# Weight tiles that start at a moving 8-byte offset, in a two-layer diffusion block

## The chip, the cores and the metric

One core of a Trainium2 chip runs the whole program. The time is the device time of one execution in microseconds; of three runs the median is taken. TensorE (PE) does the matmuls, and its weight loads (PEld) are shown as a row of their own; VectorE (DVE), ScalarE (ACT), GpSimd (POOL) and SyncE (SP, which here issues the transfers) work beside it.

## The reference

Two layers over 512 latent tokens and 256 context tokens of width 1024, in float32. Each layer is a mixer between two half-step SwiGLU FFNs, each with RMSNorms and a shift, scale and gate from a modulation vector.

```python
x = sublayer_out(x, swiglu(sublayer_in(x, g[0], mx[0], mx[1]), ffn_w_in[i, 0], ffn_w_out[i, 0]), g[1], mx[2], 0.5)
...
def swiglu(h, w_in, w_out):
    gate, up = jnp.split(h @ w_in, 2, axis=-1)     # 1024 -> 2 x 2816
    return (jax.nn.silu(gate) * up) @ w_out        # 2816 -> 1024
```

The mixer of layer 0 is a bidirectional state-space scan (SSD) in 8 groups, that of layer 1 a gated MLP (gMLP) whose gate mixes the tokens of a chunk. The first FFN and the SSD run on the context too. All of it is dominated by products of activations and weights.

## The kernel before

Every product is made of three matmuls of type fp32r: an operand is split into a high part (a rounded copy, `S.copy` in line 111) and a low part (the rest, a subtraction in line 112), and high x high, high x low and low x high are added up in PSUM. `load_w` does this for weights: it fetches 512 KB into a `raw` tile, takes two weight tiles of 128 x 1024 from `w_tile`, one for each part, and calls `split`. `mm` (line 122) issues every matmul; its second argument is the stationary operand (loaded into the array by a weight load of its own before each matmul), its third the moving one.

There are two kinds of products. In the first halves of the FFNs (`ffn_in`, by `fm_mm`), the weights are stationary and the activations move: `uh` and `ul` hold high and low part of the 512 latent tokens (8 blocks of 512 columns, 2048 bytes each), `uch` and `ucl` those of the 256 context tokens. For each of 8 blocks `fm_mm` issues high weights x `uh`, high weights x `ul`, low weights x `uh`, so that 24 matmuls use one pair of weight tiles. In the second halves (`out_gen`) the weights move in halves of 512 columns, and the stationary operand is a slice of the split hidden activations, which lie in weight tiles too (`prep_h`).

```python
for k in range(KC):
    mm(ps, wh3[:, k], uhh[:, k, lo:hi], k == 0, False)
    mm(ps, wh3[:, k], ull[:, k, lo:hi], False, False)
    mm(ps, wl3[:, k], uhh[:, k, lo:hi], False, k == KC - 1)
```

`w_tile` takes the next entry of a ring. The ring (`extra_w`) runs through the 8 buffers of tag `w` in the pool `wp` and then through n buffers of tag `w2` in a pool of the stage, 8 in the later FFNs: four weight pairs from the one and four from the other, in turn. At the end of a stage, slots of the FFN pool's `hT` tiles are used as well.

SBUF is laid out by pools, one behind another from the left (`const`, `up` with `uh` and `ul`, `rawp`, `wp`, `smp` with small tiles, `chp`, then the pools of a stage) and some from the right (`ucp` with `uch` and `ucl`, the residual stream `x`). In front of all lie 16 KiB of scratch. The order of the work is that of the code, and is not touched. Worked out from the sizes in the code, the start of a tile in its partition, modulo 512 bytes, is:

| tiles | residue before | residue after |
|---|---|---|
| `uh`, `ul` | 384 | 0 |
| weight tiles in `wp` | 384 | 8 x (5n mod 64) |
| weight tiles in the FFN pools and the pools of the last projections | 192 | 8 x (5n mod 64) |
| the one extra weight buffer in the pool of gMLP | 288 | 96 more than the others |
| `uch`, `ucl` | 480 | 0 |

n counts the weight tiles in the order in which they are taken. A weight block of 128 columns is 512 bytes, so all blocks of a tile have its residue, and so have all slices of `uh` and `ul` that a matmul reads.

Of the kernel before, what the change touches and what calls it, by code (L numbers as in the profile page):

```python
# [8 lines left out]
F32 = mybir.dt.float32  # L9
F32R = mybir.dt.float32r  # L10
# [15 lines left out]
LAG = 4  # L26
BG = 4

# order of the work on one group of SSD heads: F a piece of the next group's projections, ct/cs the
# context's chunks and states, lt/ls a latent chunk's transposes and states, d/e its decays (next  # L30
# group), a1/a2/a3 its scores, output and transposed output, p2/p3/fin what the group before left
ORDER_FIRST = """
F lt0 lt1 F ct lt2 F d0 e0 lt3 cs a10 a11 F ls0 ls3 F ls1 ls2 a20 a12 d1 e1 d2 e2 a21 F F
F F a22 d3 e3 a3 a13
# [15 lines left out]
def build(tc, I, out, upto=99):  # L50
    nc = tc.nc
# [3 lines left out]
    def pool(name, bufs=1, space=None, stack=None, side="left"):  # L55
        kw = {"side": side} if space is None else {"space": space}
        if space is not DRAM:
            kw["reuse_waits"] = "tile"
        return (stack or es).enter_context(tc.tile_pool(name=name, bufs=bufs, **kw))

    const = pool("const")
    up = pool("up")
    rawp = pool("rawp")
    wp = pool("wp")
    smp = pool("smp")
# [5 lines left out]
    def nm(s):  # L71
        cnt[0] += 1
        return f"{s}_{cnt[0]}"

    def ps_tile(tag="ps", bufs=4):
        return psp.tile([128, 512], F32, tag=tag, name=nm("ps"), bufs=bufs)

    chp = pool("chp")

    def ja(shape=(128, 1024)):  # L80
# [6 lines left out]
        return smp.tile([128, n], F32, tag=f"sm{n}", name=nm("sm"), bufs=12)  # L87

    NW = 8
    ring = [None]  # L90

    def extra_w(p, n, first=()):
        ring[0] = chain(first, cycle([(wp, "w", NW)] * NW + [(p, "w2", n)] * n))

    def w_tile(shape=(128, 1024)):
        p, tag, n = next(ring[0])
        return p.tile(list(shape), F32R, tag=tag, name=nm("w"), bufs=n)

    raws = [None]

# [13 lines left out]
    def load_w(dram, shape=(128, 1024), eng=None):  # L114
        r = raw_tile(shape)
        Q.dma_start(out=r, in_=dram)
        h, l = w_tile(shape), w_tile(shape)
        split(r, h, l, eng)
        return h, l
# [4 lines left out]
    ones = const.tile([1, 128], F32, name="ones")  # L124
# [177 lines left out]
    def out_gen(src, nch, wdram, toks, post, tail=4, bgn=0, spilled=False, banks=None, inter=None, now=99, slots=None):  # L302
# [4 lines left out]
        def prep_h(cp):  # L307
            hh, hl = w_tile((128, 2, ntok)), w_tile((128, 2, ntok))
            if spilled and cp not in spilled:
                hs = raw_tile((128, 2, ntok))  # L310
                Q.dma_start(out=hs, in_=src[cp][:, :, t0:t0 + ntok])
            else:
                hs = src[cp][:, :, t0:t0 + ntok]
            split(hs, hh, hl)
            return hh, hl
# [43 lines left out]
    def ffn_in(wdram, uhh, ull, ntok, fpool, bgn, nhalf_pairs=2, inter=None, start=None, engs=(V, V)):  # L359
# [44 lines left out]
                inter.pop(0)()  # L404
        return hts

    ucstk = ExitStack()
    ucp = pool("ucp", stack=ucstk, side="right")
    uch = ucp.tile([128, KC, CTX], F32R, name="uch")
# [12 lines left out]
    def ssd(ph, posts):  # L422
        main = ExitStack()
        sp = pool("ssd", stack=main)
# [15 lines left out]
        arow = sp.tile([128, 64], F32, name="arow")  # L440
        Q.dma_start(out=arow, in_=I["alog"].to_broadcast([128, 64]))
        S.activation(arow, arow, AF.Exp)

        def tl(shape, tag, bufs, dt=F32):
            return sp.tile(list(shape), dt, tag=tag, name=nm(tag), bufs=bufs)

        # step sizes and decays; the running sums of the latent tokens, from the middle of each
        # chunk, are kept with the tokens on the partitions (colt) and along the rows (rowd)
        colt = tl((128, NT, 2, 32), "col", 1)
        rowd = drp.tile([1, 64 * SEQ], F32, name="rowd")  # L450

        def steps_mm(hh, ll, n):
            wdh, wdl = load_w(I["ssd_wdt"].rearrange("p (k m) -> p k m", k=KC), (128, KC, 64))
            ps = ps_tile()
            for k in range(KC):
                mm(ps[:64, :n], wdh[:, k], hh[:, k, :], k == 0, False)
                mm(ps[:64, :n], wdh[:, k], ll[:, k, :], False, False)
                mm(ps[:64, :n], wdl[:, k], hh[:, k, :], False, k == KC - 1)
            return ps
# [296 lines left out]
        o = next(gen)  # L756
        next(gen)
        s = steps(px, SEQ, True)
# [10 lines left out]
        s = steps(steps_mm(uch, ucl, CTX), CTX, False)  # L769
# [17 lines left out]
        def post1(t, ps2):  # L787
            return pre_norm(xt[t], pre[:, 0, 2], uh, ul, t, post_norm(ps2, xt[t], row))

        # output projection: the first channels for the first half of the tokens while the last  # L790
        # group is under way, the others for all tokens, then the first ones for the second half
        def out_proj(o):
            n1 = 12
            ps = [[ps_tile("ps") for h in range(2)] for t in range(2)]
# [1 line left out]
            def prep_h(cp, lo, hi):  # L796
                shape = (128, 2, hi - lo)
                hh, hl = w_tile(shape), w_tile(shape)
                if cp == o.g:
                    hs = o.yt  # L800
                else:
                    hs = raw_tile(shape)
                    Q.dma_start(out=hs, in_=yts[cp][:, :, lo:hi])
                split(hs, hh, hl)
                return hh, hl
# [46 lines left out]
        for g in range(NG):  # L852
            if g + 1 < NG:
# [5 lines left out]
                prev, o = o, nxt  # L859
# [24 lines left out]
        if upto == 2:  # L884
            dump()

    # first feature tiles of the first FFN, contraction outermost so that each slice of the
    # modulation vector is used as soon as it is known
    def first_pairs(fpool, scc):
        prev = [None]  # L890
        slots = cycle([(fpool, "hT", 11)] * 11 + [(cp_, "w2", 3)] * 3)
        ring[0] = repeat((wp, "w", NW))

# [80 lines left out]
        late.extend(lambda f=f, r=r: rest(f, r) for f, r in pending)  # L974
        return [(acc[2 * f], acc[2 * f + 1]) for f in range(3)]

# [1 line left out]
    with ExitStack() as ph:  # L978
        cp_ = pool("ctxp", stack=ph)
        extra_w(cp_, 3)  # L980
# [3 lines left out]
        first = first_pairs(fpool, scc)  # L984
# [25 lines left out]
        out_phase(hts, NFP, I["ffn_out"][0], range(NTC), postc, tail=4, now=0,  # L1010
                  slots=[(fpool, "hT", 11)] * 9 + [(cp_, "w2", 3)] * 3)

# [1 line left out]
    with ExitStack() as ph:  # L1014
        ssd(ph, posts)

# [126 lines left out]
def consts():  # L1143
    import numpy as np
    i = np.arange(128)
    t, j = i[:, None], i[None, :]
    # the last two sum from the middle of a chunk, so that differences of sums lose less
    m = [t == j, t <= j, t >= j, t > j, t < j, t >= 0 * j,
         1 * ((t >= 64) & (t <= j)) - 1 * ((t > j) & (t < 64)), 1 * ((t >= j) & (t < 64)) - 1 * ((t >= 64) & (t < j))]
    return np.concatenate([np.broadcast_to(z, (128, 128)) for z in m], 1).astype(np.float32)  # L1150


def layout(inputs):
# [6 lines left out]
    R["ctx"] = A["ctx"].reshape(CTX, D)  # L1160
    R["c_ctx"] = A["c_ctx"].reshape(1, D)
    R["consts"] = consts()
    R["ada"] = A["ada_w"].transpose(0, 2, 1).reshape(2, 72, 128, D)
    R["cols"] = np.concatenate([
# [36 lines left out]

def program(arrays, upto=99):
    import concourse.bacc as _bacc
    nc = _bacc.Bacc("TRN2", target_bir_lowering=False, num_devices=1)
    I = {k: nc.dram_tensor(f"in_{k}", v.shape, mybir.dt.from_np(v.dtype), kind="ExternalInput").ap()
         for k, v in arrays.items()}
    out = nc.dram_tensor("out_0", (SEQ, D), F32, kind="ExternalOutput").ap()
    with tile.TileContext(nc) as tc:
        build(tc, I, out, upto)
    return nc  # L1210
# [8 lines left out]
```

## Time and profile before

| what | value |
|---|---|
| runs | 2600.75, 2601.16, 2601.23 us (median 2601.16) |
| span of the profiled execution | 2597.1 us |
| that execution's time | around its span, some 4 us; the page gives the span |
| TensorE, matmuls | 2537.9 us busy (98%), 12729 instructions |
| TensorE, weight loads | 2118.4 us (82%) |
| VectorE, ScalarE, GpSimd | 1535.7 us (59%), 986.4 us (38%), 339.9 us (13%) |
| mean of the granted TensorE clock | 0.995 |
| data moved | 359.09 MB, mean 138 GB/s |

The stages follow one another: the first FFN on latent tokens and then on the context to about 610 us, the SSD to 1210 us, FFN to 1560, FFN to 1940, gMLP to 2230 and the last FFN to the end. Matmuls are pipelined: one is drawn from its start until its last result, so durations overlap, and the pace is read from starts.

### The profile page before, as it was taken

The numbers are of one execution on the slowest core, as the hardware profiler recorded it, in microseconds if no ns is written. First come the engines' busy times: TensorE is split into PE (matmuls) and PEld (weight loads), VectorE is DVE, ScalarE is ACT, GpSimd is POOL, SyncE is SP. The second block draws the span as 40 slices with busy tenths as digits, with TensorE's granted clock in tenths as the row PEclk, the third lists the DMA queues.
The fourth block names the chain that finished last, engine by engine and source line by source line (L and its number), as shares of the span: only waits on it lengthen the run. The fifth ranks groups of instructions, "written<-read, shape, count | busy, mean of one in ns | idle before, by whom it ended". The sixth has DMA issues, their size and how long they took to land.

```text
span 2597.1 us, 32686 instructions
## 1 busy us (share of the span) xinstructions
PE 2537.9 (98%) x12729; PEld 2118.4 (82%) x12729; DVE 1535.7 (59%) x2224; ACT 986.4 (38%) x1464; POOL 339.9 (13%) x442
## 2 busy tenths in 40 slices
PE   5999999999899999999999999999999999999999
PEld 3888889988788888778888888888888788888887
DVE  8875547557989989977654346542342744522333
ACT  3422326446545455546222234222243323422222
POOL 5000001001545554420000000000010100000000
PEclk9999999999999999999999999999999999999999
DMA  5566545654432332345765344752333224222231
GB/s 199 191 202 206 170 146 181 201 174 138 123 91 101 97 102 90 118 162 198 238 202 168 130 130 140 234 170 73 109 111 106 81 92 136 90 98 90 81 99 63
DMA packets 131806, 359.09 MB, mean 138 GB/s; under 512 B 12234, under 2 KB 48514, under 8 KB 131652
## 3 DMA queue, kind: packets, MB, share of 16 engines
q1 hardware_dynamic: 131364, 356.82, 42.0%
q8 instruction: 100, 1.64, 0.3%
q14 instruction: 54, 0.44, 0.1%
q10 hardware_dynamic: 288, 0.19, 0.0%
HBM read 348.41 MB, written 8.55 MB: 137 GB/s over the span
## 4 chain that ended last, share of the span: by engine, by line
PE 82%; DVE 8%; DMA 3%; POOL 3%; ACT 2%; issue 1%; SPq 0%; POOLq 0%; DVEq 0%; ACTq 0%
PE ps L122 80%; DMA R<-rowd 2%; DVE acc L536 2%; DVE w L112 1%; DVE wm L671 1%; POOL R L619 1%; PE ps L269 1%; DVE ub L932 1%; POOL xs L559 0%; DVE ex L624 0%; DMA raw<-in_ssd_out 0%; POOL y L689 0%; DVE ub L570 0%; ACT w L111 0%; DVE ub L569 0%
## 5 line engine op out<-in xcount | busy, mean ns | idle before, releaser
L122 PE MATMUL ps<-uh,w 128*128 128x512 f32 (+1 forms) x3792 | 1155.1, 385 | 10.2 <-ACT uh L953 7.6
L112 DVE TENSOR_TENSOR w<-raw,w 128x1024 fp32r<-128x1024 f32 (+2 forms) x463 | 560.2, 1217 | 519.9 <-ACT w L111 342.6
L122 PEld LDWEIGHTS ps<-uh,w 128*128 128x128 f32 x3792 | 704.4, 189 | 155.3 <-ACT uh L953 8.8
L111 ACT CAST w<-raw 128x1024 fp32r<-128x1024 f32 (+2 forms) x471 | 482.1, 1032 | 905.1 <-PE ps L122 620.8
L122 PE MATMUL ps<-w,w 128*128 128x512 f32 x3144 | 729.5, 392 | 1.7 <-DVE w L112 1.5
L122 PE MATMUL ps<-ul,w 128*128 128x512 f32 (+1 forms) x1896 | 727.2, 384 | 2.6 <-DVE ul L954 2.6
L122 PEld LDWEIGHTS ps<-w,w 128*128 128x128 f32 x3144 | 587.7, 188 | 132.7 <-DVE w L112 2.8
L122 PEld LDWEIGHTS ps<-ul,w 128*128 128x128 f32 x1896 | 359.1, 189 | 78.0 <-DVE ul L954 4.8
L182 DVE CUSTOM_DVE_ANT_0 raw<-raw,sc 128x1024 f32<-128x1024 f32 x128 | 156.7, 1224 | 151.4 <-DMA raw<-in_ada 150.8
L239 POOL TENSOR_TENSOR sm<-sm,neghalf 128x1 f32<-128x1 f32 x26 | 7.2, 276 | 1601.3 <-ACT ja L237 1601.3
L122 PE MATMUL ps<-uch,w 128*128 128x256 f32 x1104 | 208.9, 286 | 0.0
L122 PEld LDWEIGHTS ps<-uch,w 128*128 128x128 f32 x1104 | 172.2, 188 | 2.6 <-issue 1.9
L122 PE MATMUL ps<-w,uh 128*128 128x256 f32 (+1 forms) x768 | 173.2, 320 | 0.0
L122 PE MATMUL ps<-ucl,w 128*128 128x256 f32 x552 | 155.6, 282 | 0.0
L536 DVE SCALAR_TENSOR_TENSOR acc<-ps,cw,acc 128x511 f32<-128x511 f32 (+2 forms) x224 | 138.5, 626 | 21.9 <-ACT acc L532 21.8
L372 DVE TENSOR_TENSOR hT<-ps,sil 128x512 f32<-128x512 f32 (+1 forms) x110 | 69.8, 634 | 112.4 <-PE ps L122 102.6
L122 PEld LDWEIGHTS ps<-w,uh 128*128 128x128 f32 x768 | 127.6, 190 | 10.4
L112 DVE TENSOR_TENSOR w<-hT,w 128x1024 fp32r<-128x1024 f32 (+1 forms) x63 | 71.2, 1130 | 96.2 <-ACT w L111 75.5
L122 PE MATMUL ps<-w,ul 128*128 128x256 f32 (+1 forms) x384 | 122.4, 319 | 0.0
L111 ACT CAST w<-hT 128x1024 fp32r<-128x1024 f32 (+1 forms) x63 | 61.1, 973 | 151.2 <-PE ps L122 151.2
L122 PEld LDWEIGHTS ps<-ucl,w 128*128 128x128 f32 x552 | 103.2, 187 | 2.0 <-issue 1.4
L371 ACT ACTIVATE sil<-ps 128x512 f32<-128x512 f32 (+1 forms) x110 | 60.8, 552 | 94.4 <-PE ps L122 94.4
(196 smaller groups left out, 1862.5 us busy)
## 6 DMA issues: line engine op xcount, KB each, us to landing
raw<-in_ffn_in SPq DMA_DIRECT2D x214, 512.0 KB, 3.8
raw<-in_ada SPq DMA_DIRECT2D x128, 512.0 KB, 4.3
raw<-in_ffn_out SPq DMA_DIRECT2D x110, 512.0 KB, 3.3
raw<-in_ssd_w SPq DMA_DIRECT2D x32, 512.0 KB, 4.5
R<-rowd SPq DMA_DIRECT2D x64, 256.0 KB, 5.0
raw<-in_ssd_out SPq DMA_DIRECT2D x28, 512.0 KB, 3.4
st<-in_ada SPq DMA_DIRECT2D x16, 512.0 KB, 7.3
raw<-in_ssd_z SPq DMA_DIRECT2D x16, 512.0 KB, 3.3
```

The source lines that it names most:

```text
L111: S.copy(out=h, in_=src)
L112: (eng or V).tensor_tensor(out=l, in0=src, in1=f32(h), op=ALU.subtract)
L122: T.matmul(o, a, b, start=start, stop=stop)
L182: V.tensor_tensor_reduce(out=r, in0=r, in1=sc, op0=ALU.mult, op1=ALU.add, scale=1.0, scalar=0.0, accum_out=mods[:, l, f:f + 1])
L239: G.tensor_tensor(out=v[:, 0:1], in0=ss[:, 0:1], in1=epsd, op=ALU.add)
L269: T.transpose(out=pt[:, k * 128:(k + 1) * 128], in_=xr[:, kk * 128:(kk + 1) * 128], identity=ident)
L371: S.activation(sil, pg[:, :ntok], AF.Silu)
L372: a = V.tensor_tensor(out=hts[-1][:, f % 2, :], in0=pu[:, :ntok], in1=sil, op=ALU.mult)
L536: V.scalar_tensor_tensor(out=acc[:, lo:hi], in0=ps[:, lo + sh:hi + sh], scalar=cw[:, j, k:k + 1], in1=acc[:, lo:hi], op0=ALU.mult, op1=ALU ...
L619: G.tensor_tensor(out=R[d], in0=R[d], in1=colt[:, c, d, gs][:, :, None].to_broadcast([128, 4, 128]), op=ALU.subtract)
L671: V.scalar_tensor_tensor(out=w1[:, h], in0=ge, scalar=sx["dt"][:, 1, c, 4 * g + h:4 * g + h + 1], in1=w1[:, h], op0=ALU.mult, op1=ALU.add)
L932: V.tensor_tensor_reduce(out=ub(), in0=r, in1=sc, op0=ALU.mult, op1=ALU.add, scale=1.0, scalar=0.0, accum_out=m0[:, f:f + 1])
```

## The change

`w_tile` allocates 128 elements (512 bytes) more than a tile needs and hands out a slice that begins o elements into the buffer, with o = 2 x (5n mod 64), that is at a multiple of 8 bytes; successive tiles are 40 bytes apart modulo 512, and 64 tiles go through all multiples of 8. Four pools get a tile that is never used, of 128, 192, 480 and 256 bytes, so that what comes after them begins at a multiple of 512 bytes. The scratch in front shrinks from 16 KiB to 1 KiB, which makes the room. Some comments are blanked.

```diff
@@ const, smp
     const = pool("const")
+    const.tile([128, 32], F32, name="padc")
...
+    smp.tile([128, 48], F32, name="pads")
     chp = pool("chp")
...
     NW = 8
+    offs = cycle(range(64))
     ring = [None]
...
     def w_tile(shape=(128, 1024)):
         p, tag, n = next(ring[0])
-        return p.tile(list(shape), F32R, tag=tag, name=nm("w"), bufs=n)
+        n1 = shape[1] if len(shape) == 2 else shape[1] * shape[2]
+        o = 2 * (next(offs) * 5 % 64)
+        z = p.tile([128, n1 + 128], F32R, tag=tag, name=nm("w"), bufs=n)[:, o:o + n1]
+        return z if len(shape) == 2 else z.rearrange("p (a b) -> p a b", a=shape[1])
...
+    pool("padr", side="right").tile([128, 120], F32, name="padx")
     ucstk = ExitStack()
...
         S.activation(arow, arow, AF.Exp)
+        sp.tile([128, 64], F32, name="padp")
...
-    nc = _bacc.Bacc("TRN2", target_bir_lowering=False, num_devices=1)
+    nc = _bacc.Bacc("TRN2", target_bir_lowering=False, num_devices=1, dynamic_dma_scratch_size=1024)
```

## Rows read from the trace of the kernel before

**Rows 1.** The page: the span, the busy time of TensorE (time, share, instructions), and the clock that TensorE was granted in 40 equal slices, in tenths, 9 being 90% or more.

```profile
span 2597.1 us, 32686 instructions
...
PE 2537.9 (98%) x12729; PEld 2118.4 (82%) x12729; DVE 1535.7 (59%) x2224; ACT 986.4 (38%) x1464; POOL 339.9 (13%) x442
...
PEclk9999999999999999999999999999999999999999
```

**Rows 2.** The page: the chain of work that ended last, its shares of the span by engine and by line.

```profile
PE 82%; DVE 8%; DMA 3%; POOL 3%; ACT 2%; issue 1%; SPq 0%; POOLq 0%; DVEq 0%; ACTq 0%
PE ps L122 80%; DMA R<-rowd 2%; DVE acc L536 2%; DVE w L112 1%; DVE wm L671 1%; POOL R L619 1%; PE ps L269 1%; DVE ub L932 1%; POOL xs L559 0%; DVE ex L624 0%; DMA raw<-in_ssd_out 0%; POOL y L689 0%; DVE ub L570 0%; ACT w L111 0%; DVE ub L569 0%
```

**Rows 3.** Groups of instructions by line, engine, operation, tiles and shape over the whole span: count | busy us, mean ns of one | idle time of the engine before them, and what ended it. Of a matmul's tiles the moving one stands first.

```profile
L122 PE MATMUL ps<-uh,w 128*128 128x512 f32 x3392 | 1079.4, 397 | 10.2 <-ACT uh L953 7.6 <-DVE w L112 2.5
L122 PE MATMUL ps<-w,w 128*128 128x512 f32 x3144 | 729.5, 392 | 1.7 <-DVE w L112 1.5
...
L122 PE MATMUL ps<-ul,w 128*128 128x512 f32 x1696 | 669.5, 395 | 2.6 <-DVE ul L954 2.6
...
L112 DVE TENSOR_TENSOR w<-raw,w 128x1024 fp32r<-128x1024 f32 x441 | 540.9, 1232 | 516.8 <-ACT w L111 339.5 <-PE ps L122 128.3 <-issue 45.4
L111 ACT CAST w<-raw 128x1024 fp32r<-128x1024 f32 x449 | 467.5, 1049 | 900.0 <-PE ps L122 617.7 <-DMA raw<-in_ffn_in 208.4 <-DMA raw<-in_ffn_out 44.5
...
L122 PE MATMUL ps<-uch,w 128*128 128x256 f32 x1088 | 205.9, 286 | 0.0
...
L122 PE MATMUL ps<-ucl,w 128*128 128x256 f32 x544 | 153.3, 282 | 0.0
...
L122 PE MATMUL ps<-w,uh 128*128 128x256 f32 x512 | 93.9, 285 | 0.0
L122 PE MATMUL ps<-w,uh 128*128 128x512 f32 x256 | 79.3, 391 | 0.0
...
L122 PE MATMUL ps<-w,ul 128*128 128x512 f32 x128 | 50.0, 390 | 0.0
```

**Rows 4.** Busy time of each engine in stretches in which PE is never idle: stretch and its length, busy us of PE, PEld, DVE, ACT, POOL with the count of instructions, granted clock, share of the DMA engines, GB/s. 1300, 1690 and 2340 us: first halves of FFNs. 1460 and 2480 us: second halves.

```profile
1300.00:1430.00 130.00, 130.00 (x567) 106.07 (x566) 62.92 (x86) 31.21 (x36) 0.00 (x0) 1.00 0.58 183
1460.00:1540.00 80.00, 80.00 (x351) 65.52 (x350) 37.82 (x39) 26.98 (x27) 0.00 (x0) 1.00 0.47 152
1690.00:1820.00 130.00, 130.00 (x568) 106.08 (x567) 48.06 (x56) 32.00 (x37) 0.00 (x0) 1.00 0.37 118
...
2340.00:2470.00 130.00, 130.00 (x567) 106.08 (x566) 36.93 (x35) 31.07 (x36) 0.00 (x0) 1.00 0.25 85
2480.00:2560.00 80.00, 80.00 (x351) 65.54 (x350) 27.47 (x23) 23.40 (x23) 0.00 (x0) 1.00 0.27 89
```

**Rows 5.** Matmuls in order of time in a first half of an FFN, on weight pairs from `wp`: start, length of the merged row, count. The first and the last of eight rows of `uh` (two matmuls each); between them lie seven threes.

```profile
1711.94 0.62 PE L122 MATMUL ps<-uh,w 128*128 128x512 f32 x2
...
1716.70 0.62 PE L122 MATMUL ps<-uh,w 128*128 128x512 f32 x2
```

**Rows 6.** The same view of the same stage, on weight pairs from the FFN's pool; six threes.

```profile
1734.55 0.63 PE L122 MATMUL ps<-uh,w 128*128 128x512 f32 x2
...
1738.75 0.63 PE L122 MATMUL ps<-uh,w 128*128 128x512 f32 x2
```

**Rows 7.** The same view where weight tiles of two residues (288 and 384) are used in turn. From 1962.89 us in gMLP's first product, where the weights move and `uh`, `ul` are stationary: eight threes, then tiles of residue 384 alone from 1968.46. From 2074.41 us in gMLP's second product, where the weights are stationary: six threes.

```profile
1962.89 0.63 PE L122 MATMUL ps<-w,uh 128*128 128x512 f32 x2
...
1968.46 0.62 PE L122 MATMUL ps<-w,uh 128*128 128x512 f32 x2
...
1969.85 0.62 PE L122 MATMUL ps<-w,uh 128*128 128x512 f32 x2
...
1970.53 0.62 PE L122 MATMUL ps<-w,uh 128*128 128x512 f32 x2
...
2074.41 0.39 PE L122 MATMUL ps<-ul,w 128*128 128x512 f32 x1
...
2078.57 0.39 PE L122 MATMUL ps<-ul,w 128*128 128x512 f32 x1
```

**Rows 8.** A stretch of the SSD at a lower granted clock (the number before the last two), and the matmuls in it in order of time.

```profile
699.80:702.20 2.40, 2.40 (x7) 1.92 (x6) 2.40 (x4) 0.55 (x1) 2.40 (x2) 0.50 0.64 220
...
700.18 0.63 PE L122 MATMUL ps<-ul,w 128*128 128x512 f32 x1
...
701.46 0.63 PE L122 MATMUL ps<-ul,w 128*128 128x512 f32 x1
```

**Rows 9.** The page: the busiest DMA queue and its kind, packets, MB, share of 16 engines' time.

```profile
q1 hardware_dynamic: 131364, 356.82, 42.0%
```

**Rows 10.** A stretch of the SSD, columns as in rows 4.

```profile
650.00:780.00 130.00, 119.82 (x708) 102.58 (x708) 117.00 (x220) 66.59 (x102) 64.96 (x69) 0.96 0.37 109
```

**Rows 11.** Groups as in rows 3, between 650 and 1170 us (the SSD): the matmuls that are 512 wide.

```profile
L122 PE MATMUL ps<-uh,w 128*128 128x512 f32 x473 | 161.5, 410 | 2.5 <-DVE w L112 2.5
L122 PE MATMUL ps<-ul,w 128*128 128x512 f32 x237 | 94.0, 397 | 0.0
...
L122 PE MATMUL ps<-w,w 128*128 128x512 f32 x256 | 63.4, 400 | 0.1
```

**Rows 12.** Matmuls in order of time in the first FFN on the context, 256 wide: from 423.47 us on a weight pair from `wp` (14 threes), from 432.27 us on a pair from the FFN's pool (8 threes).

```profile
423.47 0.28 PE L122 MATMUL ps<-ucl,w 128*128 128x256 f32 x1
...
428.51 0.28 PE L122 MATMUL ps<-ucl,w 128*128 128x256 f32 x1
...
432.27 0.28 PE L122 MATMUL ps<-ucl,w 128*128 128x256 f32 x1
...
435.08 0.28 PE L122 MATMUL ps<-ucl,w 128*128 128x256 f32 x1
```

## The prediction, made before the result was known

> **What bounds the kernel now.** I read the page first: TensorE is busy 98% of a span of 2597.1 us at full granted clock in all 40 slices as the page rounds them [rows 1], and the chain that ended last is matmuls for four fifths of its length [rows 2]. So the question is not which wait is removed (the change removes none) but what one matmul costs, and whether the place of its operands in SBUF enters into that cost. The groups by shape give the counts: 5088 matmuls 512 columns wide with `uh` or `ul` moving, 3528 of the same width with a weight tile moving (3144 + 256 + 128), some 3000 that are 256 wide [rows 3]. Their mean durations overlap, so the pace is taken from stretches in which PE never idles, as time by count (one of the count is cut by the edge): 130 us / 566 = 229.7 ns in the first halves of three FFNs, 80 us / 350 = 228.6 ns in the second halves of two [rows 4]. Weighted by the counts that is 229.2.
>
> Then I took single weight tiles apart in the timeline, where `uh` x2 and `ul` x1 come in threes. Seven threes take 4.76 us on one tile pair, 226.7 ns a matmul [rows 5]; six threes take 4.20 us on a pair used 22 us later, 233.3 ns [rows 6]. Both stretches are inside one stage, with the same instructions, at full clock. What differs is the buffers: the ring hands out four pairs from `wp` and then four from the FFN's pool, and the pace flips with it, every four pairs. By the layout in the kernel section, the first pair lies at the same place modulo 512 bytes as `uh` and `ul` (384), the second 192 bytes off (192). A third stretch shows two weight tiles of different residues used in turn: eight threes take 5.57 us, 232.1 ns, and then, back to tiles of one residue, two threes take 1.39 us (231.7 ns) before the next takes 0.68 us (226.7); six threes with the stationary tiles in turn at 288 and 384 take 4.16 us, 231.1 ns [rows 7].
>
> One more row says what the extra is. Where the granted clock was 0.50 (1.2 GHz), three matmuls take 1.28 us from start to start, 426.7 ns each [rows 8]: 512 columns at 1.2 GHz and nothing else. At 2.4 GHz the columns alone would be 213.3 ns; 226.7 is 13.3 over, 233.3 is 20 over. So a matmul pays 13 to 20 ns beside its columns, and the amount depends on how the moving stream and the load of the next weights lie to each other. I read it as two streams from one memory that get in each other's way; if they lie alike they settle into the cheapest pattern seen, and if they don't, or if it changes from tile to tile, they don't settle.
>
> [...]
>
> **The change, part by part.** *Padding.* 128 bytes in `const`, 192 in `smp`, 480 on the right side and 256 in `ssd` move `uh`, `ul`, `uch`, `ucl` and the bases of the weight pools to residue 0. No instruction is added (the padding tiles are never written). Cost nothing by itself.
>
> *Scratch from 16 KiB to 1 KiB.* It makes room for 512 more bytes in each weight buffer. What it could cost is a queue that needs it; every data transfer goes through hardware queues and the main one held 42% of the engines' time [rows 9]; no queue of a software kind is listed. Cost nothing; if it did bind, transfers would come late, and there is no row to price that from but the slack of ScalarE, which waits for free buffers (617.7 us for PE) three times as long as for the FFN's weights (208.4 us) [rows 3].
>
> *Writing the shifted tiles.* ScalarE's cast (1049 ns) and VectorE's subtraction (1232 ns) of a 128x1024 tile [rows 3] now write and read at 8-byte steps. In the FFN stages VectorE is busy 37 to 63 of 130 us [rows 4], so that PE covers any small growth. The cover is thin in the SSD stage (117 of 130 us) [rows 10], where a growth of 1% would be 12 ns on each of some fifty tiles: under 1 us. I take nothing.
>
> *Matmuls and weight loads on shifted tiles.* This is where the time is decided. The tiles now start at 40n modulo 512 bytes, so high and low part of a pair always lie 40 bytes apart, and over 64 tiles every multiple of 8 is used once. `uh` and `ul` stay at 0. Hence the settled case of rows 5 (all residues equal) goes away in the dense stages, as does the settled dear one of rows 6; what remains is the case of rows 7, residues that change between loads, in every tile. I take the middle of its two rows, 231.6 ns.
>
> - `uh`/`ul` moving: 5088 less the 710 of the SSD stage [rows 11] is 4378, from 229.7 to 231.6: 4378 x 1.9 = +8.3 us.
> - weights moving: 3528 less 256 is 3272, from 228.6 to 231.6: 3272 x 3.0 = +9.8 us.
> - the 966 of the SSD stage at +2.5 make 2.4 us; PE was idle 10 of 130 us in its worst stretch [rows 10] and waits on others there, so I charge half: +1.2 us.
> - 256 wide: today 120.0 ns (14 threes in 5.04 us), and 117.1 ns (8 threes in 2.81 us) on tiles of another residue [rows 12]. Both are the same instructions, so either can come; I take no change, with 3000 x -2.9 = -9 us as the lower bound and, if they pay in proportion as the wide ones do (1 ns), +3 us as the upper.
>
> Bounds for the wide ones: all 8616 settled as in rows 5 is 8616 x (226.7 - 229.2) = -22 us; all as dear as rows 6 is 8616 x (233.3 - 229.2) = +35 us. With the 256-wide ones: -31 to +38.
>
> What no row shows is an operand that is not on a multiple of 32 bytes. [...]
>
> **Sum.** 8.3 + 9.8 + 1.2 = +19 us. The profiled execution's span of 2597.1 us lies 4.1 us under the median of the runs, 2601.16, as start and end lie outside it; nothing in the change touches these. 2601 + 19 = 2620 us, 0.7% slower. Between two versions I call 0.2% (5 us) about the least that can be told from no change.
>
> **Rivals.**
> *Each tile settles anyway (faster).* If only the relative timing of the two streams mattered, each new tile would drift to the 226.7 ns of rows 5, as the tile after the mixed ones did within two threes. The dear pairs of rows 6 would be gone, and the time would be 2601 - 22 = 2579, or 2590 with half of the tiles so. The price decides at a mean of 229.2 ns: under it the change gains. Against it: the pairs of rows 6 had a whole stage and never left 233.3. Chance 18%.
> *The offset changes nothing.* What rows 5 to 7 show could be owed to which pools are used (far apart or near) and not to residues, or the mean over 64 residues could just equal today's mix, 229.2. [...] Time 2596 to 2606. Chance 15%.
> *Off-line starts are dear.* If a load from an odd multiple of 8 bytes needed each piece twice, the 13.3 ns over the columns would double on the low parts, a third of the matmuls: 8616 / 3 x 13.3 = +38 us on top of +19, 2658. For it: nothing. Against: `uch` at 480, half a step off 64, was not dearer [rows 12]. Chance 7%.
> *The forecast:* residues that change keep the streams unsettled, 2607 to 2643. Chance 60%.
>
> **From chances to numbers.** Slower than 2606: 60 + 7 = 67%; within 0.2%: 15%; faster: 18%. The range from 2592 to 2643 leaves out the better half of the first rival (some 11%) and the last one. The forecast's own range is 2607 to 2643.
>
> **What would show it.** The pace in the FFNs' first halves: 230.5 to 232.5 ns in place of 229.7, and no longer flipping every four pairs; second halves the same. Durations on VectorE and ScalarE unchanged; PE's idle time unchanged; the transfer queues unchanged. The reading is wrong if single tiles show a pace under 226, or if many tiles settle at 226.7: then it is time and not place that matters. It is wrong in kind if the pace stays and the span moves.

## The result, and the profile after

The changed kernel takes 2614.98 us (median of 4 runs, 2614.01 to 2616.48) where the kernel before, on the same chip, took 2600.95 (2599.49 to 2601.23): 14.0 us slower, a ratio of 1.0054 [1.004, 1.0069]. The spans of the profiled executions are 2613.0 and 2597.1 us [rows 1]. In the listed runs an execution takes 2.0 us more than its span (2614.98 for the one of 2613.0), not the 4.1 us of the prediction: the profiled execution of the kernel before was some 2 us quicker than its median, and so the spans lie 15.9 us apart where the medians lie 14.0 apart.

The page of the changed kernel: span, engines, busiest queue, and the chain that ended last by engine.

```profile
span 2613.0 us, 32685 instructions
...
PE 2555.5 (98%) x12729; PEld 2116.4 (81%) x12729; DVE 1537.7 (59%) x2224; ACT 985.5 (38%) x1464; POOL 338.6 (13%) x442
...
q1 hardware_dynamic: 131364, 356.82, 40.3%
...
PE 83%; DVE 8%; POOL 2%; DMA 2%; ACT 2%; issue 1%; SPq 0%; POOLq 0%; DVEq 0%; ACTq 0%
```

The same 12729 matmuls keep TensorE busy 17.6 us longer, in a span 15.9 us longer; no other engine's busy time grows by more than 2 us. The groups by shape say the same of the work around them (columns as in rows 3; the change moved line 122 to 128, 111 to 117 and 112 to 118):

```profile
L128 PE MATMUL ps<-uh,w 128*128 128x512 f32 x3392 | 1086.4, 399 | 9.7 <-ACT uh L961 7.5 <-DVE w L118 2.2
L128 PE MATMUL ps<-w,w 128*128 128x512 f32 x3144 | 737.8, 395 | 1.3 <-DVE w L118 1.1
...
L128 PE MATMUL ps<-ul,w 128*128 128x512 f32 x1696 | 673.7, 397 | 2.6 <-DVE ul L962 2.6
...
L118 DVE TENSOR_TENSOR w<-raw,w 128x1024 fp32r<-128x1024 f32 x441 | 540.5, 1232 | 537.8 <-ACT w L117 339.7 <-PE ps L128 133.3 <-issue 61.3
L117 ACT CAST w<-raw 128x1024 fp32r<-128x1024 f32 x449 | 466.7, 1047 | 893.5 <-PE ps L128 663.5 <-DMA raw<-in_ffn_in 172.3 <-DMA raw<-in_ffn_out 28.5
```

VectorE's subtraction (1232 ns) and ScalarE's cast (1047) last what they did, TensorE's waits before these matmuls are the same within 1 us, and ScalarE waits less for transfers than before, not more. The three dense groups of matmuls take 19.5 us more busy time. In stretches without idle time (columns as in rows 4):

```profile
1300.00:1430.00 130.00, 130.00 (x562) 105.41 (x561) 62.54 (x85) 30.12 (x35) 0.00 (x0) 1.00 0.55 184
1460.00:1540.00 80.00, 80.00 (x347) 64.88 (x346) 37.13 (x38) 25.73 (x26) 0.00 (x0) 1.00 0.44 151
1690.00:1820.00 130.00, 130.00 (x563) 105.42 (x562) 49.21 (x59) 31.40 (x36) 0.00 (x0) 1.00 0.38 129
2340.00:2470.00 130.00, 130.00 (x562) 105.44 (x561) 37.73 (x36) 30.89 (x36) 0.00 (x0) 1.00 0.25 85
2480.00:2560.00 80.00, 80.00 (x348) 64.81 (x347) 30.32 (x27) 24.71 (x25) 0.00 (x0) 1.00 0.31 105
```

Counted as the prediction counts, first halves go from 229.7 to 130 us / 561.3 = 231.6 ns a matmul and second halves from 228.6 to 80 us / 346.5 = 230.9, at a granted clock of 1.00. Single tiles still differ. Matmuls in order of time in two first halves of the changed kernel; `ul` stands once in every three:

```profile
1747.13 0.39 PE L128 MATMUL ps<-ul,w 128*128 128x512 f32 x1
...
1751.94 0.40 PE L128 MATMUL ps<-ul,w 128*128 128x512 f32 x1
1753.33 0.39 PE L128 MATMUL ps<-ul,w 128*128 128x512 f32 x1
...
1757.53 0.39 PE L128 MATMUL ps<-ul,w 128*128 128x512 f32 x1
...
2289.96 0.39 PE L128 MATMUL ps<-ul,w 128*128 128x512 f32 x1
...
2294.76 0.40 PE L128 MATMUL ps<-ul,w 128*128 128x512 f32 x1
```

Over the first two rows lie seven threes on a pair at offsets 240 and 280: 4.81 us / 21 = 229.0 ns. Over the next two lie six threes on the next pair, at 320 and 360: 4.20 us / 18 = 233.3. So the pace goes on depending on the tile. Over the last two lie seven threes on a pair of another FFN, at 496 and 24, 256 bytes from the first: 4.80 us / 21 = 228.6. Cut into stretches of seven threes on one pair (from the first row of `ul` to the eighth), the trace gives 194 without a stall, from 227.3 to 233.7 ns: one rounds to 227, 12 to 229, 73 to 231, 60 to 232, 40 to 233 and 8 to 234. The place decides among them: taken to the nanosecond, all 11 pairs whose high part lies at 240 or 496 run at 228.8 to 228.9 ns, and all 10 at 224 or 480 at 233.2 to 233.7.

### The profile page after: what moved, and what is told of

It is laid out like the page before. It is cut to its first block, busy times and chain, and to the rows that moved or that the text cites. A ratio compares the mean times of both kernels' runs of the same rounds, so it can differ in the third digit from the quotient of the medians.

```text
span 2613.0 us, 32685 instructions
## 1 busy us (share of the span) xinstructions
PE 2555.5 (98%) x12729; PEld 2116.4 (81%) x12729; DVE 1537.7 (59%) x2224; ACT 985.5 (38%) x1464; POOL 338.6 (13%) x442
## 4 chain that ended last, share of the span: by engine, by line
PE 83%; DVE 8%; POOL 2%; DMA 2%; ACT 2%; issue 1%; SPq 0%; POOLq 0%; DVEq 0%; ACTq 0%
PE ps L128 82%; DVE acc L544 2%; DMA R<-rowd 2%; DVE w L118 1%; DVE wm L679 1%; PE ps L275 1%; POOL R L627 1%; DVE ub L940 1%; POOL xs L567 0%; DVE ex L632 0%; DMA raw<-in_ssd_out 0%; POOL y L697 0%; DVE ub L578 0%; PE ps L552 0%; ACT w L117 0%
## 5 line engine op out<-in xcount | busy, mean ns | idle before, releaser
L128 PE MATMUL ps<-w,w 128*128 128x512 f32 x3144 | 737.8, 395 | 1.3 <-DVE w L118 1.1
```

What stands on the lines that cost most here:

```text
L128: T.matmul(o, a, b, start=start, stop=stop)
```

## The experiments

The change has two halves that can be run apart: the padding, which brings every operand to the same place, and the offsets, which scatter the weight tiles again. All runs below compute the whole reference. "Residue" is a tile's start modulo 512 bytes. The table gives, beside the times, the mean from one matmul's start to the next in the traces, over all matmuls of a width but those next to a stall or at the lower clock (some 8470 of those 512 wide, 2938 of those 256 wide); "u" means `uh` or `ul` moving over weight tiles, "w" a weight tile moving over another.

| kernel | median us | ratio to before | 512 wide: u, w | all 512 wide | 256 wide |
|---|---|---|---|---|---|
| before | 2601 | | 229.45, 228.83 | 229.16 | 119.59 |
| changed | 2614.98 | 1.0054 [1.004, 1.0069] | 231.76, 231.58 | 231.68 | 118.37 |
| e1_zero | 2584.53 | 0.9937 [0.9922, 0.9951] | 227.07, 226.99 | 227.09 | 119.76 |
| e2_pairs | 2619.72 | 1.0072 [1.0055, 1.0089] | 231.81, 232.56 | 232.14 | 118.27 |
| e3_scratch | 2601.78 | 1.0005 [0.9996, 1.0014] | | 229.14 | 119.58 |
| e4_320 | 2607.33 | 1.0025 [1.0015, 1.0034] | 233.29, 227.03 | 230.82 | 116.76 |
| e5_best | 2581.29 | 0.9922 [0.991, 0.9935] | | 227.07 | 118.07 |
| e6_376 | 2603.12 | 1.0006 [0.9997, 1.0015] | 226.9, 233.8 | 229.75 | 119.71 |
| e7_pad | 2583.97 | 0.9937 [0.9922, 0.9953] | | 227.06 | 119.85 |
| e8_next | 2612.49 | 1.0045 [1.0032, 1.0059] | | 231.35 | 117.73 |
| e9_common | 2614.94 | 1.0051 [1.0031, 1.0071] | 231.93, 230.9 | 231.59 | 117.2 |
| e10_best | 2577.01 | 0.991 [0.9894, 0.9927] | | 227.08 | 116.80 |
| e11_low320 | 2613.38 | 1.0044 [1.0028, 1.006] | 231.1 (w) | 231.17 | 117.93 |

### The padding without the offsets

```diff
-        o = 2 * (next(offs) * 5 % 64)
+        o = 0
```

> The changed kernel with its padding, its longer weight buffers and its small scratch, but every weight tile at offset 0: moving and stationary tiles all have residue 0 (but one buffer of gMLP). Theory A (the pace follows the residues of the two streams; equal ones settle at 226.7 ns): the 512-wide matmuls, 8470 of them not next to a stall, go from 231.7 ns in the changed kernel to 227.3 (with a few unsettled at each tile's start), 8470 x 4.4 = 37 us; the 256-wide go from 118.4 to 119.8, +4 us: 2582 us, 19 us (0.7%) below the kernel before. Theory B (starts that are no multiple of 64 bytes cost something by themselves; residues that agree or not don't matter): only the change's own loss goes, about 2601. Theory C (the padding or the scratch cost the time): stays at 2615.

Measured: 2584.53 us, 16.5 under the kernel before and 30.5 under the changed one. Two stretches (a first half, a second half; columns as in rows 4):

```profile
1690.00:1820.00 130.00, 130.00 (x575) 107.55 (x574) 45.83 (x53) 32.19 (x37) 0.00 (x0) 1.00 0.37 121
...
2480.00:2560.00 80.00, 80.00 (x354) 66.24 (x353) 25.83 (x25) 20.62 (x26) 1.05 (x4) 1.00 0.27 86
```

130 us / 574 = 226.5 and 80 us / 353 = 226.6 ns (one matmul more or less in the count is 0.4 to 0.6 ns): the pace of rows 5 everywhere. The offsets alone cost 30.5 us; the padding, with the scratch and the longer buffers, gains 16.5. That is also the answer to the rival by which only pools matter and not places: the pools are the same in both kernels, and only a number in the offset differs.

### One unused tile in the kernel before

```diff
+    smp.tile([128, 48], F32, name="pads")
     chp = pool("chp")
```

> The kernel before with one unused tile of 192 bytes in smp and nothing else: the FFN pools move from residue 192 to 384, that of uh, ul and the other weight tiles. Theory A: all 512-wide matmuls settle at 226.7, mean 227.1 in place of 229.2; 8470 x 2.1 = 18 us less: 2583, as with offset 0. If the whole of the change's padding is needed: 2601.

Measured: 2583.97 us, pace 227.06. The 192 bytes that no instruction touches bring the FFN's pool to the residue of `uh` and `ul`, and that alone is worth 17 us. The dear pairs of rows 6 are that residue and nothing else.

### The smaller scratch alone

```diff
-    nc = _bacc.Bacc("TRN2", target_bir_lowering=False, num_devices=1)
+    nc = _bacc.Bacc("TRN2", target_bir_lowering=False, num_devices=1, dynamic_dma_scratch_size=1024)
```

> The kernel before with the scratch of 1 KiB alone (all tiles move by 15 KiB, no residue changes). Theories A and B: no change, 2601 within 3 us. Theory C, if it is the scratch that costs: some of the 14 us by which the changed kernel is slower.

Measured: 2601.78 us, ratio 1.0005 [0.9996, 1.0014]. No cost can be told from none: the interval leaves room for 0.14%, some 4 us.

### Both tiles of a pair at one offset

```diff
-    offs = cycle(range(64))
+    offs = cycle(range(128))
-        o = 2 * (next(offs) * 5 % 64)
+        o = 2 * (next(offs) // 2 * 5 % 64)
```

> The changed kernel, but high and low tile of a pair get the same offset, and the offset moves on by 40 bytes from pair to pair. Theory A in its form 'what changes from load to load keeps the streams unsettled': within 24 matmuls with uh and ul moving, the residue now stands still, so each pair settles: at 226.7 ns where it is 0 or 256 bytes off, elsewhere at its own value between 226.7 and 233.3, on the mean some 230, 5 us per 3000 matmuls less than the changed kernel: 2605 to 2611. Theory A in the form 'the residue alone decides': as the changed kernel, 2615 within 3. Theory B: as the changed kernel, 2615.

Measured: 2619.72 us, above every time expected and a little dearer than the changed kernel, though each 24 matmuls now use one residue. Matmuls in order of time, a pair at offset 56 (first two rows) and one at 376 (last two), seven threes each:

```profile
1705.96 0.39 PE L128 MATMUL ps<-ul,w 128*128 128x512 f32 x1
...
1710.87 0.40 PE L128 MATMUL ps<-ul,w 128*128 128x512 f32 x1
...
1750.35 0.39 PE L128 MATMUL ps<-ul,w 128*128 128x512 f32 x1
...
1755.11 0.39 PE L128 MATMUL ps<-ul,w 128*128 128x512 f32 x1
```

4.91 us / 21 = 233.8 ns (233.3 to the nanosecond) and 4.76 us / 21 = 226.7. The pace does settle within a pair, nearly always on a value that goes with its residue, and most values are dear: of 194 such stretches 104 lie at 233 ns or above, 61 between 230 and 233, 10 at 228 to 229 and 19 below. 226.7 came at 0 and 256 (after some matmuls), 40 and 296, 120 and 376, and once at 496; the other pairs at 240 and 496 took 228.4. Residues 256 apart behave alike, with a few strays: of two pairs at 40, one ran at 226.7 and the other at 233.2 from end to end. So where a pair has one residue, "unsettled" is not the right word for a shifted tile; "settled, mostly dear" is. And the mean with `u` moving, 231.81 ns, is the changed kernel's 231.76, although no offset changes within a pair here: that high and low part lie 40 bytes apart is not needed for the loss.

### All weights at 320

```diff
-        o = 2 * (next(offs) * 5 % 64)
+        o = 80
```

> The changed kernel with every weight tile at a constant offset of 320 bytes: uh and ul moving are 192 above the weights modulo 512, as in the dear stretches of the kernel before, and weights moving over weights agree. Theory A: 4990 matmuls with uh or ul moving settle at 233.3 ns (229.5 in the kernel before: +19 us), 3100 with weights on weights at 227.3 (228.8 before: -5 us), the others within 2 us: 2615, 14 us slower than before, though no tile's place changes. Theory B (320 is a multiple of 64): as offset 0.

Measured: 2607.33 us. A first half and a second half, columns as in rows 4:

```profile
1690.00:1820.00 130.00, 130.00 (x559) 104.75 (x558) 47.83 (x56) 31.02 (x36) 0.00 (x0) 1.00 0.38 122
...
2480.00:2560.00 80.00, 80.00 (x355) 66.23 (x354) 29.55 (x25) 24.48 (x24) 0.00 (x0) 1.00 0.32 106
```

With `u` at 0 and weights at 320, 130 us / 558 = 233.0 ns; with weight tiles moving over weight tiles, both at 320, 80 us / 354 = 226.0. So here alike is cheap (226.0) and 64 apart modulo 256 is dear (233.0), as said. The time was to be 2615 and came out 8 us lower, because the 256-wide matmuls gained 2.8 ns each (119.59 to 116.76; 2.8 x 2938 = 8 us), which the expectation had not priced.

Where the granted clock falls to 0.50, the dear place is no dearer than the cheap one. A stretch of the SSD in this kernel, and matmuls in it in order of time, six from the first row to the second:

```profile
700.50:703.20 2.70, 2.70 (x8) 2.05 (x7) 2.70 (x5) 0.69 (x1) 2.70 (x2) 0.50 0.64 200
...
700.57 0.63 PE L128 MATMUL ps<-ul,w 128*128 128x512 f32 x1
...
703.13 0.63 PE L128 MATMUL ps<-ul,w 128*128 128x512 f32 x1
```

2.56 us / 6 = 426.7 ns with `u` at 0 and weights at 320, as with equal residues in rows 8.

### All weights at 376

```diff
-        o = 2 * (next(offs) * 5 % 64)
+        o = 94
```

> The changed kernel with every weight tile at a constant offset of 376 bytes, no multiple of 16. Theory A (residues of the two streams, period 256): in the sweep over pairs all five tile pairs at 376 ran at 226.7 ns with uh and ul moving; weights over weights agree (226.7): as with offset 0, 2585 within 4 us. [...]

Measured: 2603.12 us where 2585 was expected, so the theory that only the difference of the two starts counts falls. The same two stretches show where:

```profile
1690.00:1820.00 130.00, 130.00 (x575) 107.48 (x574) 48.06 (x56) 31.77 (x37) 0.00 (x0) 1.00 0.38 122
...
2480.00:2560.00 80.00, 80.00 (x343) 64.47 (x342) 27.38 (x23) 23.35 (x23) 0.00 (x0) 1.00 0.28 92
```

Weights loaded from 376 under a moving tile at 0 are as cheap as any here (130 us / 574 = 226.5 ns). Weight tiles at 376 moving over others at 376, difference zero, take 80 us / 342 = 233.9. So a start at 376, an odd multiple of 8 bytes, shows no cost in the weight loads and some 7 ns in the moving tiles.

### One offset per step in the second halves

```diff
-        o = 2 * (next(offs) * 5 % 64)
+        o = 2 * (step_[0] * 5 % 64)
```

(`step_[0]` goes up by one with each step of the FFN, so that moving and stationary tiles of a step in the second half share a residue; in the first halves it goes up with each pair, so that high and low part share one.)

> The changed kernel, but in the FFNs the offset moves on once per step of the loop: in the second halves the activations' tiles and the two weight pairs of a step share one residue (48 matmuls), and the next step has another. [...] Theory A (only the difference counts): 226.7 at every residue. The run with 376 speaks against A. Time: between 2590 and 2610.

Measured: 2614.94 us; the range expected was missed because the first halves, where `u` stays at 0, stayed at 231.93 ns, and the second halves came to 230.9 on the mean, against the changed kernel's 231.58. The second halves show which starts are cheap. Each row below is the matmuls of one step in one piece, in order of time, at offsets 208, 248, 288 and 328:

```profile
1463.90 10.79 PE L128 MATMUL ps<-w,w 128*128 128x512 f32 x46
...
1474.99 10.88 PE L128 MATMUL ps<-w,w 128*128 128x512 f32 x46
...
1486.17 10.82 PE L128 MATMUL ps<-w,w 128*128 128x512 f32 x47
...
1497.05 11.11 PE L128 MATMUL ps<-w,w 128*128 128x512 f32 x47
```

Taking the last matmul's 0.39 us off each length: 10.40 / 45 = 231.1 ns at 208 (16 over a multiple of 32), 10.49 / 45 = 233.1 at 248 (an odd 8), 10.43 / 46 = 226.7 at 288 (a multiple of 32), 10.72 / 46 = 233.0 at 328. Over the steps of the FFNs that run in one piece: 227.1 at multiples of 32 (436 matmuls), 231.1 at 16 over (412), 233.0 at odd multiples of 8 (871). Theory A's 226.7 at every residue did not come: where the weights start alike, the moving fp32r tiles of this run are cheapest on multiples of 32 bytes, and a start 16 bytes over one takes 4 ns more. That it is the moving tile's start that costs, and not the load's, is shown at 376 alone (e6_376: 226.5 ns loaded, 233.9 moving).

### Two residues in turn, arranged and not arranged

```diff
-        o = 2 * (next(offs) * 5 % 64)
+        o = 80 * (next(offs) % 2)
```

High parts lie at 0 and low parts at 320, both multiples of 64. In e11_low320 all activations stay at 0. In e8_next `ul` and `ucl` are moved to 320 too, so that each moving tile agrees with the weights that are loaded while it streams.

> The changed kernel with high tiles at offset 0, low tiles at 320, ul and ucl moved to residue 320 too. Each moving tile then agrees with the weights that are loaded for the next matmul while it streams, but in two of three matmuls not with its own weights (320 or 192 off). If the streams that meet are a matmul's moving tile and the load for the next one: all at 226.7, 2585 us. If it were the relation to its own weights: two of three at 233.3, the mean 231.1, 2585 + 8470 x 4.0 = 2619.

> The changed kernel with high tiles at offset 0, low tiles at 320, uh, ul, uch, ucl at 0. With uh and ul moving, the moving residue never changes and one weight load in three is 320 off the stream that it meets. If each matmul is priced by its own meeting: two at 226.7 and one at 233.3, 228.9 on the mean, 2594 us. If a residue that changes from load to load keeps the whole sequence from settling: about 231.4, as with ul at 320, and 2605 to 2612.

Measured: 2612.49 us for e8_next, between the two times expected, and 2613.38 for e11_low320, a little above the 2605 to 2612 of its second case. A first half and a second half of e8_next:

```profile
1690.00:1820.00 130.00, 130.00 (x564) 105.70 (x563) 49.22 (x58) 31.10 (x36) 0.00 (x0) 1.00 0.39 126
...
2480.00:2560.00 80.00, 80.00 (x348) 64.98 (x347) 29.46 (x27) 25.55 (x25) 0.00 (x0) 1.00 0.32 106
```

130 us / 563 = 230.9 ns, neither the 226.7 of "each agrees with its load" nor 233.3. In e11_low320 the three matmuls of a triple take 228.5, 229.2 and 235.5 ns on average, 231.1 together, where two cheap meetings and one dear one would make (2 x 226.7 + 233.3) / 3 = 228.9. So a matmul can't be priced by its own moving tile and its own load: with residues that change from load to load the mean stood at 231.1 to 231.4 ns in these two runs; what sets it there, no run shows. The changed kernel's 231.7 is only 0.5 ns above e11_low320's 231.2, although half of its weight tiles start on odd multiples of 8 and none do here. That does not clear the starts off a multiple of 32: in the second halves of e9_common they bring 230.9 with no change of residue within a step. Each of the two is enough for most of the loss there, and no run shows their shares.

### A version that beats both

e5_best is e1_zero with the 256-wide operands set apart: `uch` and `ucl` at 168, the weights `ssd_z` and the first two pairs of each FFN at 64. e10_best takes `uch` and `ucl` back to 0 and instead starts the weight tiles of the context's FFN at 88. "The line" in its expectation stands for multiples of some number of bytes on which a moving tile has to start; the ground for it is e6_376, where tiles at 376 were cheap to load (226.5 ns) and dear to move (233.9).

```diff
-    def w_tile(shape=(128, 1024)):
+    def w_tile(shape=(128, 1024), o=0):
...
-                    w = load_w(wdram[2 * f + j], eng=engs[j])
+                    w = load_w(wdram[2 * f + j], eng=engs[j], o=22 if ntok == CTX else 0)
...
-            wz = [load_w(I["ssd_z"][g, i], eng=WL[4 + i]) for i in range(2)]
+            wz = [load_w(I["ssd_z"][g, i], eng=WL[4 + i], o=16) for i in range(2)]
```

> Padding and small scratch as in the changed kernel; all weight tiles at offset 0 (512-wide matmuls at 226.7 ns, as in the run with offset 0), but where 256-wide matmuls use them the residues are taken from the sweep over pairs: uch and ucl lie at 168 (113.5 ns there, 119.7 at equal residues), the z weights of the SSD and the first two pairs of an FFN at 64 (117.8 and 115.6 ns, 119.8 at equal ones). Theory A: 2584.5 - 1620 x 6.2 - 560 x 4.2 - half of 750 x 2.0 = 2571 us, 1.2% below the kernel before. If the 256-wide pace in the sweep was owed to the tiles around and not to the residue: 2584.

> As the kernel with residues chosen for the 256-wide matmuls, but uch and ucl back at residue 0, and the weight tiles that meet them in the context's FFN at 88 (in the sweep over pairs 256-wide matmuls ran at 113.5 ns where the weights lay at 88 modulo 256). Theory D (the moving tile must be on the line, the weights may be anywhere): 1056 matmuls at 113.5 in place of 119.9, 6.8 us less than that kernel's 2581: 2574. If it was the tiles around: 2581.

Measured: 2581.29 us for e5_best, 10 us above the 2571 expected: the 1620 matmuls with `uch` or `ucl` moving took 119.9 ns in place of 113.5 (the lowest pace seen for 256 wide, on one pair of e2_pairs with the weights at 168; one at 424 took 120.0 there). 168 is no multiple of 32; that this is the reason is argued from e10_best, where the difference of the starts is the same modulo 256 and the moving tile is back at 0. It took 2577.01 us, 24.6 under the kernel before, ratio 0.991 [0.9894, 0.9927], between the 2574 and the 2581 expected, and is the fastest kernel seen here. Its context FFN, 256 wide, in order of time, first 14 threes and then 15:

```profile
413.04 0.28 PE L127 MATMUL ps<-ucl,w 128*128 128x256 f32 x1
...
417.80 0.28 PE L127 MATMUL ps<-ucl,w 128*128 128x256 f32 x1
...
419.02 0.28 PE L127 MATMUL ps<-ucl,w 128*128 128x256 f32 x1
...
424.27 0.28 PE L127 MATMUL ps<-ucl,w 128*128 128x256 f32 x1
```

4.76 us / 42 = 113.3 ns, then 5.25 us / 45 = 116.7, with the same residues. So one layout ran at two paces. The first holds on two pairs, the second on the 42 pairs after them; what decides between them, no run shows.

## Why the prediction was right, and where a step was off

**The direction and the mechanism.** 14 us slower came where +19 was forecast, with 2620 against 2615 measured. That the place of the operands sets the pace is shown by e1_zero, and that alike operands settle near 226.7 ns by e1_zero (all at 0, mean 227.09) and e7_pad (all at 384, mean 227.06). The step that is not borne out is the reason for the new pace: that offsets which change from load to load keep the streams from settling. In the changed kernel pairs do settle, nearly all on a pace that goes with their residue (228.8 ns at 240 and 496, some 233.6 at 224 and 480). And the same means come where nothing changes within a pair or a step: 231.81 with `u` moving in e2_pairs (231.76 in the changed kernel), 230.9 with weights moving in e9_common (231.58). Residues in turn do cost about as much by themselves (e8_next and e11_low320, 231.1 to 231.4), but that the mean over 64 residues lies there too, the forecast did not know. So its 231.6 ns, taken from rows 7, is met within 0.2 ns by luck in part.

**The wide terms.** `u` moving: 4378 x (231.76 - 229.45) = +10.1 us, against +8.3. Weights moving: 3272 x (231.58 - 228.83) = +9.0, against +9.8. With those of the SSD stage, all 8470 without a stall: 8470 x 2.52 = +21.3 us; the three terms said 19.3.

**The term that was wrong.** The 256-wide matmuls were taken at no change, inside bounds of -9 to +3 us. They went from 119.59 to 118.37 ns: 2938 x -1.2 = -3.5 us. Rows 12 had a pair at 120.0 and one at 117.1, and the kernel before was nearly all at the dear one; by these two rows a mix lowers the mean. To take no change where most stood at the dearer of the two was the fault. The sum is then 21.3 - 3.5 = +17.8 us, and the span grew by 15.9. The rest lies in the SSD, where TensorE waits for others and for which the prediction halved a term. From 615 to 1230 us, in the kernel before and in the changed one (columns as in rows 4):

```profile
615.00:1230.00 615.00, 593.38 (x3471) 499.72 (x3470) 541.50 (x965) 330.19 (x567) 254.51 (x300) 0.99 0.37 117
...
615.00:1230.00 615.00, 595.36 (x3478) 498.77 (x3477) 540.64 (x962) 332.57 (x571) 253.72 (x302) 0.99 0.36 116
```

TensorE's idle time there falls from 21.6 to 19.6 us.

**The costs put at nothing.** The scratch: e3_scratch shows no cost beyond the noise. Writes at shifted addresses: shown by the unchanged durations (1232 and 1047 ns). The padding costs no instruction, but "nothing by itself" hides that it is worth -16.5 us (e1_zero); the prediction went from today's mix straight to the new one and so needed no price for it.

**The rivals.** *Each tile settles anyway* is half right, which the forecast had not seen: tiles do settle within 24 matmuls, in e2_pairs and in the changed kernel. It falls on the pace they settle at: in e2_pairs 226.7 for few residues and 230 or more in 165 of 194 stretches, and in the changed kernel 231 to 234 in 181 of 194. *The offset changes nothing* falls by e1_zero, 30.5 us away with only the offset taken out. The same instructions at the same granted clock (1.00) take 226.5 ns with the weights at 376 (e6_376) and 233.0 with them at 320 (e4_320). *Off-line starts are dear* was argued against with `uch` at 480, which is a multiple of 32 and so no test of it. The effect exists for moving tiles (e6_376, e9_common: +4 and +6 to 7 ns), and in the changed kernel all low parts, which move in the second halves, lie on odd multiples of 8. It does not show for weights loaded from 376 (e6_376, 226.5 ns), and nowhere does it reach the 13.3 ns that the 2658 us need.

**What was to show it.** Pace in the first halves 230.5 to 232.5: 231.6. Second halves "the same": 230.9. The flip every four pairs is gone, and the pace changes from pair to pair in its place. Durations and queues as before: yes; idle time, 2 us less. No tile under 226, and not many at 226.7: of 194 stretches none, and one at 227.3.

**What stays open.** That the moving stream and the weight load get in each other's way is the author's reading, and no run shows it. What the runs show is that the pace depends on both starts (weights at 376 take 226.5 ns under a tile at 0 and 233.9 under one at 376, e6_376; weights at 320 take 233.0 under a tile at 0, e4_320), and that at a granted clock of 0.50 it is 426.7 ns at equal [rows 8] and at unequal residues (e4_320). The traces give the clock as a share of full speed; the prediction's 1.2 and 2.4 GHz stand for the column rate of rows 8, 512 columns in 426.7 ns or 1.2 a ns at 0.50, and for twice that rate at 1.00. Its 213.3 ns for the columns is half of 426.7, an estimate, and so are the 13.3 and 20 ns beside them: they take the 426.7 ns to be columns alone, for which the equal time at both residues speaks. How much of the changed kernel's loss is owed to dear residues, to starts off a multiple of 32 and to residues in turn was not separated. Why starts 40 and 120 bytes apart are as cheap as equal ones (226.7 ns in e2_pairs), and why one layout has two paces (113.3 and 116.7 ns in e10_best, 226.7 and 233.2 at 40 in e2_pairs), was not settled.

## What to carry to other kernels

Where TensorE is busy nearly all the time (98% here), take the pace of single tiles from the timeline: if equal matmuls differ by tile, look at the starts of the operands. In these runs the 512-wide fp32r matmuls were cheapest with moving and weight tiles at one residue (a mean of 227.06 ns at 384 in e7_pad and of 227.09 at 0 in e1_zero) that is a multiple of 32 bytes (227.1 ns against 231.1 and 233.0 in e9_common): try such a place first. Here one unused tile of 192 bytes did it, for 17 us of 2601. Don't spread starts over all residues: that averages good and dear places, and in e2_pairs 165 of 194 stretches took 230 ns or more.

## What the runs showed of the hardware that had not been expected

- The pace of a 512-wide fp32r matmul with its weight load ranged from 226.7 to 234.3 ns with the residue of the weights, alike 256 bytes apart (226.7 at 0 and 256, 40 and 296, 120 and 376) but for a few pairs (e2_pairs). At a granted clock of 0.50 it was 426.7 ns at equal and at dear residues (rows 8, e4_320).
- Where the weights start alike, a moving fp32r tile was cheapest on multiples of 32 bytes: 227.1, 231.1 (16 over) and 233.0 ns (odd multiples of 8) in e9_common. Weight tiles loaded from 376 under a moving tile at 0 took 226.5 ns, as cheap as at 0 (e6_376, e1_zero).
- 256 wide, the best place seen is not the same one: 119.8 ns at equal residues (e1_zero), 113.3 and 116.7 with the weights 88 bytes on (e10_best).
- Two residues in turn cost more than a mix of the two paces alone: 231.1 ns against 228.9 (e11_low320).
